# Two gate projections as seven-product block problems, branches and merge with tokens as rows, and the mixer put in a new order

## The chip, the cores and the metric

The kernel runs on one core of a Trainium2 chip. The metric is device time in microseconds for one execution. In a profile, PE is TensorE's matmuls, PEld its weight loads, DVE is VectorE, ACT is ScalarE, POOL is GpSimd and SP is SyncE, which here only issues DMAs.

## The reference

Two layers (`DEPTH = 2`) of a streaming encoder over 512 tokens of width 1024, all in float32. Each layer is a token mixer and then a SwiGLU FFN, both with a residual and a layer norm behind them. The mixer, cut to what the change touches:

```python
h = jnp.einsum('bsd,de->bse', x, w_in[l])
rq, rk, rv, rg, cq, ck, cv, dq, dk, dv, gates = jnp.split(h, splits, axis=-1)   # gates: 3 x 1024 columns
o_a = _retention(rq, rk, rv, rg, ...)          # 4 heads, values 256 wide: 1024 columns
o_b = _chunk_attention(cq, ck, cv, ...)        # 8 heads of 64: 512 columns
o_c = _diff_attention(dq, dk, dv, ...)         # 4 heads of 2 x 64: 512 columns
g = sigmoid(gates + b_merge[l])                # one gate per branch and channel
merged = g_a * (o_a @ w_branch_a[l]) + g_b * (o_b @ w_branch_b[l]) + g_c * (o_c @ w_branch_c[l])
x = layer_norm(ALPHA * x + merged @ w_out[l])
```

Here the heads' shapes and the slices of `gates` are abridged. The gate projection is the widest piece: three matrices of 1024 x 1024 on 512 tokens. The kernel takes the sigmoid as (tanh(z/2) + 1)/2, and folds the factor 1/2 into a later copy.

## The kernel before

**Precision.** Every float32 operand is carried as a pair (`Pair`): a high part in float32r (ACT's cast) and the remainder (DVE's subtraction). One product is three matmuls (`mm3`, lines 121 to 124): high x high, high x low, low x high. A matmul has 128 x 128 stationary and up to 512 moving columns.

**Weights.** A weight block of 2048 columns per partition (1 MB) is loaded by SP into one of four staging slots (`wst`), cast by ACT (L154, L312), its remainder taken by DVE (L155, L319), into one of three slots for split weights (`wsp`). `run_items` walks a list of items written out by hand; `AHEAD = 3` blocks are fetched ahead of the item that runs.

**Items and gaps.** An item is a pair of weight requests and a function that issues its matmuls; the groups written behind it are lists of small steps, one list run at each call of `between()`, which the items make between their output tiles. The steps are the DVE, ACT and attention work: `s_q` (quarter sums), `s_r1` to `s_r3` (retention), `s_c1` to `s_c3` (chunk attention), `s_d0` to `s_d4` (differential attention). A planner orders each engine's queue by its own costs, with the program's order as priority; `keep_in_program_order` and `issue_after` bind single instructions.

**Two forms of projection.** The plain form, `proj_T`, makes a tile with 128 output channels as rows and 512 tokens as columns, in 24 matmuls for a depth of 1024. The block form, `u_two`, takes a weight matrix of 1024 x 1024 as 2 x 2 blocks of 512, the activations as halves of tokens by halves of depth, and forms the result from seven block products, named m1, m2, y, v, x, g, h, instead of eight, each 24 matmuls; its output has tokens as rows. Some products take plain quarters of the activations (m1, m2, h), the others sums of quarters, which `Quarters.left` (y and x) and `Quarters.right` (v and g) prepare from `xf` for four tiles k (`s_q(k)`: the tiles `sa` and `s12`, `sb` and `s43`). Weights are summed as well: `ahead_a` loads a block and has POOL's DMA add a second onto it, `ahead_c` the same; the classes `Close` and `Early` differ in how the other sums are made on DVE (L251, L257, L280). Before the change the block form serves the values `CV`/`DV` (`w`), two pairs of retention values and gates (`p`, `q`), the output projection (`o`) and the FFN.

**Gates and merge before.** The three gate matrices are in the plain form: `u_gate(br, i)` makes two tiles of channels; `gate_done` takes tanh with the bias as a per-partition scalar (L1121). Ten of the 24 tiles of a layer (`EARLY`) are parked in DRAM and come back later. `u_branch(br, i)` makes two tiles of channels of a branch's projection and merges them (L1154, L1158) into `acc[d]`, which has channels as rows, just what the output projection wants as its activation. Its quarter sums are `s_mleft` and `s_mright`.

**Order in a layer.** Layer 0 starts with `u_first` (retention's first queries and keys, and gate tiles 0 and 1, six tiles), two gate items, then `w`'s products. Layer 1 starts with m1 and m2 of `w`, whose plain quarters need no sums, while the previous layer's norm is turned; then `u_first`, with the steps `natural` (two operations on each half of a token tile's residual row, L579 and L580) and `s_q` in its gaps, two gate items, and then `w["y"]`. Behind that come `p` and `q`, and then attention steps in the gaps of branch, gate and query/key items. Gate items of 48 matmuls stand all along the mixer.

## Time and profile before

| | |
|---|---|
| time, median of 3 runs | 1864.18 us (1863.9 to 1864.31) |
| profiled execution: span | 1862.2 us, 2.0 us under the median; its own time beyond the span is not recorded |
| PE, DVE, ACT, POOL busy | 99%, 75%, 53%, 7% of the span |
| matmuls | 8772 |
| mean granted TensorE clock | 0.999 |
| moved by DMA | 302.89 MB, 163 GB/s in the mean |

"Busy" is the share of the span in which an engine has at least one instruction under way. A row of a group gives the line, the engine, the operation, the tiles written and read, the shapes and the count; then busy time and mean duration in ns; then the idle time of the engine just before, and what ended it. A matmul's duration overlaps its neighbours', so what one more matmul costs is the distance between two starts. Layer 0's mixer runs from 0 to about 586 us, its FFN to about 940, layer 1's mixer to about 1513.

### The profile page before, as it was taken

Reading aid. Unit: us, or ns where it says so; the run is one execution under the profiler, and the core shown is the slowest. Engines: PE = TensorE matmul, PEld = TensorE weight load, DVE = VectorE, ACT = ScalarE, POOL = GpSimd, SP = SyncE. Lnnn points to the kernel's source line nnn. Section 1 sums busy time; section 2 is a strip of 40 time slices with the busy share of each in tenths; the row PEclk is TensorE's granted clock in tenths of the full one; section 3 lists DMA queues with packets and bytes.
Section 4 is the critical chain, followed back from the end, with each engine's and each line's share of the span. In section 5 each row is a group of like instructions: output and inputs, shape, how many; then the busy total and the mean of one; then the engine's idle time right before and its main releaser. Section 6 shows DMA issues by size and latency. Waiting matters only on the chain.

```text
span 1862.2 us, 23357 instructions
## 1 busy us (share of the span) xinstructions
PE 1852.4 (99%) x8772; PEld 1547.1 (83%) x8772; DVE 1391.9 (75%) x2124; ACT 990.1 (53%) x1590; POOL 131.1 (7%) x151
## 2 busy tenths in 40 slices
PE   9999999999999999999999999999999999999998
PEld 8888888888888888888888888888888888888887
DVE  6867756677679777888686777566775897778886
ACT  5555545576545445554354545546665464455540
POOL 2000000000001100010010000000000011000100
PEclk9999999999999999999999999999999999999999
DMA  9685444332456777797376844433325477777871
GB/s 285 189 262 152 124 139 133 95 121 75 121 167 166 179 198 182 202 220 205 129 227 186 257 115 143 152 110 106 113 68 147 137 181 183 198 198 198 202 197 46
DMA packets 235426, 302.89 MB, mean 163 GB/s; under 512 B 8757, under 2 KB 127633, under 8 KB 235313
## 3 DMA queue, kind: packets, MB, share of 16 engines
q1 hardware_dynamic: 205888, 244.09, 40.7%
q0 software_dynamic: 29280, 57.05, 17.6%
q8 instruction: 69, 1.13, 0.2%
q14 instruction: 45, 0.36, 0.1%
q10 hardware_dynamic: 144, 0.26, 0.0%
HBM read 279.29 MB, written 22.07 MB: 162 GB/s over the span
## 4 chain that ended last, share of the span: by engine, by line
PE 97%; DVE 2%; issue 0%; ACT 0%; POOL 0%; DVEq 0%; POOLq 0%
PE pt L122 15%; PE pt L123 15%; PE pt L124 15%; PE pf L124 14%; PE pf L122 14%; PE pf L123 14%; PE ptr L487 1%; PE psc L458 1%; PE pco L1002 1%; PE psc L457 1%; PE ph L1365 1%; PE pdo L1074 1%; DVE wl L155 1%; PE pro L124 1%; PE pro L123 1%; PE pro L122 1%
## 5 line engine op out<-in xcount | busy, mean ns | idle before, releaser
L319 DVE TENSOR_TENSOR wl<-st,wh 128x2048 fp32r<-128x2048 f32 (+1 forms) x143 | 320.5, 2244 | 118.5 <-ACT wh L312 117.9
L122 PE MATMUL pt<-xTh,wh 128*128 128x512 f32 x960 | 377.3, 394 | 0.0
L123 PE MATMUL pt<-xTl,wh 128*128 128x512 f32 x960 | 374.0, 390 | 0.4 <-DVE xTl L112 0.4
L124 PE MATMUL pt<-xTh,wl 128*128 128x512 f32 x960 | 374.2, 390 | 0.0
L312 ACT CAST wh<-st 128x2048 fp32r<-128x2048 f32 x140 | 267.3, 1912 | 194.0 <-PE pf L124 97.0
L155 DVE TENSOR_TENSOR wl<-st,wh 128x1024 fp32r<-128x1024 f32 (+2 forms) x186 | 200.2, 1093 | 48.6 <-ACT wh L154 35.2
L154 ACT CAST wh<-st 128x1024 fp32r<-128x1024 f32 (+2 forms) x186 | 172.2, 949 | 115.9 <-PE pt L123 56.1
L124 PEld LDWEIGHTS pt<-xTh,wl 128*128 128x128 f32 x960 | 180.2, 188 | 38.0
L123 PEld LDWEIGHTS pt<-xTl,wh 128*128 128x128 f32 x960 | 180.4, 188 | 37.0 <-DVE xTl L112 0.8
L122 PEld LDWEIGHTS pt<-xTh,wh 128*128 128x128 f32 x960 | 180.7, 188 | 36.5 <-ACT xTh L106 0.2
L122 PE MATMUL pf<-wh,xTh 128*128 128x512 f32 x336 | 132.0, 393 | 0.2
L124 PE MATMUL pf<-wh,xTl 128*128 128x512 f32 x336 | 131.6, 392 | 0.3
L123 PE MATMUL pf<-wl,xTh 128*128 128x512 f32 x336 | 130.9, 390 | 0.0
L122 PE MATMUL pf<-wh,s12h 128*128 128x512 f32 x256 | 100.7, 393 | 0.0
L122 PE MATMUL pf<-wh,s43h 128*128 128x512 f32 x256 | 99.8, 390 | 0.0
L123 PE MATMUL pf<-wl,s12h 128*128 128x512 f32 x256 | 99.8, 390 | 0.0
L123 PE MATMUL pf<-wl,s43h 128*128 128x512 f32 x256 | 99.7, 389 | 0.0
L124 PE MATMUL pf<-wh,s43l 128*128 128x512 f32 x256 | 99.4, 389 | 0.0
L124 PE MATMUL pf<-wh,s12l 128*128 128x512 f32 x256 | 99.2, 390 | 0.0
L809 ACT COPY tc<-pf 128x512 f32<-128x512 f32 x84 | 48.4, 589 | 80.6 <-PE pf L124 77.4
L124 PEld LDWEIGHTS pf<-wh,xTl 128*128 128x128 f32 x336 | 63.1, 188 | 15.4 <-DVE xTl L112 2.5
L122 PEld LDWEIGHTS pf<-wh,xTh 128*128 128x128 f32 x336 | 63.1, 188 | 14.0 <-issue 1.0
(329 smaller groups left out, 3666.7 us busy)
## 6 DMA issues: line engine op xcount, KB each, us to landing
st<-in_w_in SPq DMA_DIRECT2D x53, 1024.0 KB, 5.7
st<-in_w_ffn_in SPq DMA_DIRECT2D x38, 1024.0 KB, 5.6
st<-in_w_in SPq DMA_DIRECT2D x48, 512.0 KB, 5.1
st<-in_w_ffn_out SPq DMA_DIRECT2D x22, 1024.0 KB, 7.0
st<-in_w_ffn_in POOLq DMA_DIRECT2D x20, 1024.0 KB, 10.8
st<-in_w_ffn_out POOLq DMA_DIRECT2D x16, 1024.0 KB, 9.0
st<-in_w_in POOLq DMA_DIRECT2D x12, 1024.0 KB, 11.6
st<-in_w_ffn_in SPq DMA_DIRECT2D x24, 512.0 KB, 5.3
```

Of the source, the lines that this page charges most:

```text
L122: nc.tensor.matmul(ps, lh, rh, start=start, stop=False, skip_group_check=onto)
L123: nc.tensor.matmul(ps, lh, rl, start=False, stop=False, skip_group_check=onto)
L124: nc.tensor.matmul(ps, ll, rh, start=False, stop=stop, skip_group_check=onto)
L154: return [nc.scalar.copy(self.hi[:, a:b], self.st[:, a:b]), nc.vector.tensor_sub(self.lo[:, a:b], self.st[:, a:b], f(self.hi[:, a:b]))]
L155: nc.vector.tensor_sub(self.lo[:, a:b], self.st[:, a:b], f(self.hi[:, a:b]))]
L312: nc.scalar.copy(self.hi, st)
L319: nc.vector.tensor_sub(self.lo[:, k], self.st[:, k], f(self.hi[:, k]))
L457: nc.tensor.matmul(ps[:, :w], self.q[j][:, n], self.k[j][:, :w], start=True, stop=False)
L458: nc.tensor.matmul(ps[:, :w], self.q[j][:, n], self.kl[j][:, :w], start=False, stop=True)
L487: nc.tensor.transpose(ps[:, o + P * (nt - mt):o + P * (nt - mt) + P], E[pk][:, c + P * mt:c + P * mt + P], ident)
L809: nc.scalar.copy(t[to, j], ps)
L1002: nc.tensor.matmul(*x, start=mt == 0 and x is hi, stop=mt == NT - 1 and x is hi)
```

## The change

Gate matrices 0 and 1 go into the block form (`u_gates`, seven products each), with a bias row added at the copy; their tanh tiles have tokens as rows. Gate 2 and the three branches are made in `strips`: the activation is the stationary operand, 512 weight columns move, and the result has tokens as rows. All 24 tanh tiles of a layer go to DRAM and return at the merge. Merged tiles are turned by 32 transposes per layer (`s_merged`), and the output projection's sums are taken behind that (`s_msums`). `u_first` loses its gate block; in layer 0 and layer 1 the two gate items ahead of `w["y"]` make room for m1 and m2 of the first gate; `vectors`, `lam`, `v_back` and the split of `ob` move; `held` tells the fetch loop that strips keep a block longer.

```diff
-                while at <= i or (at < len(items) and sum(map(len, ready)) < AHEAD):
+                while at <= i or (at < len(items) and held + sum(map(len, ready)) < AHEAD):
...
-            return [([wcols(c, 256)], KT) for c in (RQ, RK, GATE)], fn
+            return [([wcols(c, 256)], KT) for c in (RQ, RK)], fn
...
                 def use(j, ps):
                     t[to, j] = g(name="t" + to)
-                    nc.scalar.copy(t[to, j], ps)
+                    if base:
+                        nc.vector.tensor_add(t[to, j], ps, base[to])
+                    else:
+                        nc.scalar.copy(t[to, j], ps)
...
             def h(j, ps):
+                if base:
+                    c, ps = ps, g(name="th")
+                    nc.vector.tensor_add(ps, c, base["c11"])
                 left_done(2 + j, ps)
...
+        def gate_done(br, hf, t, c):
+            nc.scalar.activation(c, c, AF.Tanh, scale=0.5)
+            th[br, t, hf] = dram.tile([P, 512], F32, name=f"th{l}_{br}_{t}_{hf}")
+            nc.sync.dma_start(th[br, t, hf], c)
...
+        def u_gates(kind, br):
+            hv = kind(W, 0, 4, (GATE + D * br, GATE + D * br + 512))
+            return u_two(hv, xq, functools.partial(gate_done, br, 0), functools.partial(gate_done, br, 1), Rows(br))
+
+        def strip(act, ks, wt, t, ps=None, stop=True):
+
+            start, sl = ps is None, slice(P * t, P * t + P)
+            ps = bank("pn") if start else ps
+            for i, k in enumerate(ks):
+                mm3(ps, act[k].hi[:, sl], act[k].lo[:, sl], wt.hi[:, i], wt.lo[:, i],
+                    start and i == 0, stop and i == len(ks) - 1)
+            return ps
...
+        def merge(br, t, hf, ps):
+            s = g(name="th")
+            nc.sync.dma_start(s, th.pop((br, t, hf)))
+            nc.vector.scalar_tensor_tensor(s, s, 1.0, ps, op0=ALU.add, op1=ALU.mult)
+            if (t, hf) in acc:
+                nc.vector.tensor_add(acc[t, hf], acc[t, hf], s)
+            else:
+                acc[t, hf] = s
...
+        def s_merged(half, *ks):
+
+            def fn():
+                for k in ks:
+                    ps = bank("pm")
+                    for hf in range(2):
+                        for j in range(2):
+                            o = 256 * hf + P * j
+                            nc.tensor.transpose(ps[:, o:o + P], acc[2 * half + j, hf][:, P * k:P * k + P], ident)
+                    r = raw[half, k] = g(name="mr")
+                    nc.scalar.activation(r, ps, AF.Copy, scale=0.5)
...
+        def s_msums(*ks):
+
+            def fn():
+                for k in ks:
+                    a, b, y = raw.pop((0, k)), raw.pop((1, k)), raw.pop(("y", k))
+                    pr, gr = Pair("mx"), HalfPair("mg")
+                    nc.vector.tensor_sub(y[:, A2], y[:, A2], a[:, A2])
+                    nc.vector.tensor_add(y[:, B2], y[:, A2], a[:, B2])
+                    split(pr, y)
+                    mq[k].put("x", pr, A2)
+                    mq[k].put("v", pr, B2)
+                    nc.vector.tensor_sub(a[:, A2], a[:, A2], b[:, A2])
+                    split(gr, a[:, A2])
+                    mq[k].put("g", gr, A2)
...
+        ga, gb = u_gates(Early, 0), u_gates(Close, 1)
...
         if l == 0:
-            start = [(u_first(),), (u_gate(0, 1), [s_q(0), s_q(1)], [s_q(2), w["a"]]), (u_gate(0, 2), [s_q(3)], [w["c"]]),
-                     (w["m1"],), (w["y"],), (w["v"],), (w["m2"], [lam])]
+            start = [(u_first(), [w["a"]], [s_rows(0)]), (w["m1"], [vectors, s_q(0)], [s_q(1)]), (w["m2"], [s_q(2)], [w["c"]]),
+                     (ga["m1"], [s_q(3)]), (ga["m2"], [lam])]
         else:
             turned, natural = ([functools.partial(fn, i) for i in range(4)] for fn in hooks[l])
             start = [(w["m1"], [ret_tables], turned[:2]), (w["m2"], turned[2:]),
-                     (u_first(), [natural[0]], [natural[1]], [natural[2]], [natural[3], w["a"]], [s_q(0)]),
-                     (u_gate(0, 1), [s_q(1)], [s_q(2)]), (u_gate(0, 2), [s_q(3)], [w["c"]]),
-                     (w["y"], [lam]), (w["v"],)]
+                     (u_first(), [natural[0]], [natural[1]], [natural[2], s_rows(0)], [natural[3], w["a"]]),
+                     (ga["m1"], [vectors, s_q(0)], [s_q(1)]), (ga["m2"], [s_q(2), w["c"]], [s_q(3), lam])]
...
+            (w["y"], [ga["a"]]), (w["v"],), (w["x"],), (w["g"],), (ga["y"],), (w["h"], [ga["c"]]), (ga["v"], [gb["a"], s_rows(1)]),
+            (ga["x"],), (gb["m1"],), (ga["g"],), (gb["y"],), (ga["h"], [gb["c"]]), (gb["v"], [p["a"]]), (gb["m2"], [s_dh(0)]), (gb["x"],),
+            (p["m1"],), (gb["g"],), (p["y"],), (gb["h"], [p["c"]], [s_r1(0)]), (p["v"], [s_dh(1)]), (p["m2"], [], [s_r1(1)]),
...
+            (u_cqk(2), [s_c2(1), s_c1(3)], [s_c3(1), s_c2(2)]),
+            a0[0], a0[1], (u_cqk(3), 2, [s_c3(3), s_c2(4)], [s_c3(4), s_c1(6)]), a0[2], a0[3],
+            a1[0], a1[1], (u_dqk(0), 2, [], [s_d0(0, 0)]), a1[2], a1[3],
+            (u_dqk(1), [s_d2(0), s_ob(0, 1)], [s_d0(1, 0), s_ob(2, 3)]), (u_chunked(0), [s_d3(0)], [s_d0(1, 1)]),
+            (u_dqk(2), [s_d4(0), s_d2(1)], [s_d0(2, 0)]), g1[0], g1[1],
+            (u_dqk(3), 2, [s_d4(1), s_d2(2)], [s_d0(3, 0)]), g1[2], g1[3],
+            (u_chunked(1), [s_d4(2), s_d2(3), o["a"]], [s_d3(3)]),
+            *quad(difference_strips(s_d4(3)), [], [[o["c"]]], [[], [s_merged(1, 0, 1)]], [[s_merged(1, 2, 3)]]),
+            (o["y"], [s_merged(0, 0, 1, 2, 3)]), (o["m1"], [s_msums(0)], [s_msums(1)]), (o["m2"], [s_msums(2)], [s_msums(3)]),
+            (o["v"],), (o["x"], [norm_rows]),
             (o["g"], [], [s_turned(0)]), (o["h"],),
```

More of the change, by code (lines that the diff above doesn't have):

```diff
@@ L588, in last_of, with item @@
         return [next(own) for _ in range(n)][-1]
[L590 to L592 removed]
+    def item(specs, fn, *groups, held=0):
+        items.append((specs, fn, groups, held))
     pending = []
@@ L931, in v_away, with v_back @@
             return done
-        def v_back(dst):
+        def v_back(dst, hf):
             def fn():
-                for k, away in list(dst.items()):
-                    dst[k] = g(F32R, "vhl")
-                    nc.sync.dma_start(f(dst[k]), away)
+                for t in range(NT):
+                    away, dst[t, hf] = dst[t, hf], g(F32R, "vhl")
+                    nc.sync.dma_start(f(dst[t, hf]), away)
             return fn
@@ new lines, in strip, with strips, part, fn @@
+        def strip(act, ks, wt, t, ps=None, stop=True):
[5 more added lines that the diff above has]
+            return ps
+        def strips(act, w, hf, use):
+            W2, ps = {}, {}
+            def part(k, ts):
+                def fn(*wt):
+                    if wt:
+                        W2[k], = wt
+                    for t in ts:
+                        if k == 0:
+                            ps[t] = strip(act, range(0, 4), W2[0], t, stop=False)
+                        else:
+                            use(t, hf, strip(act, range(4, 8), W2[1], t, ps.pop(t)))
+                return fn
+            c = slice(512 * hf, 512 * hf + 512)
+            one, two = [([w[0:512, c]], 4)], [([w[512:1024, c]], 4)]
+            return [(one, part(0, (0, 1)), 0), (two, part(1, (0, 1)), 1), ([], part(0, (2, 3)), 2), ([], part(1, (2, 3)), 1)]
```

202 lines of the change are left out of this document (91 added, 111 removed).

## The prediction

> **What bounds the kernel now.** I read the page first (busy shares and the chain that ended last), then the busy time in stretches of my own choice, then the instructions in order of time of PE and DVE round the stage that the change rebuilds.
>
> ```profile
> span 1862.2 us, 23357 instructions
> ...
> PE 1852.4 (99%) x8772; PEld 1547.1 (83%) x8772; DVE 1391.9 (75%) x2124; ACT 990.1 (53%) x1590; POOL 131.1 (7%) x151
> ...
> PE 97%; DVE 2%; issue 0%; ACT 0%; POOL 0%; DVEq 0%; POOLq 0%
> ```
>
> TensorE is the bound: it is busy 99% of the span and carries 97% of the chain. A matmul that goes is worth its spacing, as long as its operands stay ahead of PE. Whether they do is a question of stretches (columns: stretch, length, then busy time and count of PE, PEld, DVE, ACT, POOL, the clock, the DMA share and GB/s):
>
> ```profile
> 29.53:67.23 37.70, 37.70 (x168) 31.24 (x167) 31.29 (x46) 20.87 (x28) 2.64 (x2) 1.00 0.75 207
> 942.18:1002.57 60.39, 59.98 (x263) 48.64 (x261) 51.71 (x80) 29.52 (x45) 8.66 (x14) 1.00 0.73 209
> 235.50:551.00 315.50, 315.43 (x1590) 266.77 (x1589) 214.60 (x468) 183.47 (x396) 16.04 (x22) 1.00 0.41 122
> 551.00:561.90 10.90, 10.90 (x50) 9.03 (x49) 10.90 (x13) 5.50 (x5) 0.00 (x0) 1.00 0.32 97
> 69.00:240.00 171.00, 170.86 (x804) 143.16 (x803) 129.21 (x151) 92.76 (x134) 8.20 (x8) 1.00 0.62 183
> ```
>
> PE has no hole in any of them. In the first two, the openings of layers 0 and 1 up to the last quarter sum, DVE is busy 83% and 86%. That matters because the first product that needs quarter sums (`w["y"]`) cannot finish before DVE has written `s12` for the fourth tile. The rows in time, layer 0 and then layer 1:
>
> ```profile
> 60.49 0.39 PE L122 MATMUL pf<-wh,xTh 128*128 128x512 f32 x1
> ...
> 65.93 0.39 PE L122 MATMUL pf<-wh,s12h 128*128 128x512 f32 x1
> ```
> ```profile
> 29.53 0.69 DVE L424 TENSOR_TENSOR rot<-pt,cosr 128x512 f32<-128x512 f32 x1 [3.54 <-DMA cosr<-in_rope_ret]
> ...
> 66.62 0.68 DVE L112 TENSOR_TENSOR s12l<-sa,s12h 128x512 fp32r<-128x512 f32 x1
> ```
> ```profile
> 997.85 0.39 PE L122 MATMUL pf<-wh,s12h 128*128 128x512 f32 x1
> ...
> 1002.71 0.50 PE L124 MATMUL pf<-wh,s12l 128*128 128x512 f32 x1
> ```
> ```profile
> 1001.97 0.68 DVE L112 TENSOR_TENSOR s12l<-sa,s12h 128x512 fp32r<-128x512 f32 x1
> ```
>
> In layer 1, PE enters `y` at 997.85, runs all that does not need the fourth tile, and takes its low part at 1002.71, just after DVE wrote it (1001.97 + 0.68). The slack is nil. In layer 0 the fourth tile is finished at 67.3 and `y` would use it at 65.93 + 9 matmuls = 68.0. So in both layers the work that PE has ahead of `y` now is just enough to cover DVE. This decides my forecast.
>
> **The change, part by part.** *Matmuls.* Between 60.49 and 65.93 lie the 24 matmuls of one product: 5.44 us, 0.2267 each. A gate matrix is now 8 column tiles x 8 x 3 = 192 matmuls; as seven products of 24 it is 168. Two matrices, two layers: 96 fewer, -21.8 us. The third gate, the branches and the output projection keep their counts (2 halves x 4 token tiles x 8 x 3 = 192, as before).
>
> *Transposes of merged tiles.* 4 x 2 x 4 = 32 per layer, 64 in all.
>
> ```profile
> 253.57 1.04 PE L912 MATMUL prt<-ident,ro 128*128 128x128 f32 x8
> 254.37 0.48 PE L122 MATMUL pt<-xTh,wh 128*128 128x512 f32 x1
> ```
>
> Eight take 0.80 us from start to start: 64 cost +6.4 us, all on PE. PE's own account is thus -15.4 us. I would expect 8772 - 96 + 64 = 8740 matmuls.
>
> *The opening of each layer.* This is the part on the path. Layer 0 now has 264 matmuls ahead of `y` (six tiles of `u_first`, two gate items, `w["m1"]`); after, 192 (four tiles, and m1 and m2 of `w` and of the first gate). That is 72 x 0.2267 = 16.3 us less cover: PE reaches `y` at 49.6. Layer 1 goes from 288 to 192, 21.8 us less: at 976.1. From there 18 of the 24 matmuls can run without the fourth tile (as the order of layer 1 shows today), 4.1 us more: 53.7 and 980.2. What has DVE to do until then? Its prices:
>
> ```profile
> L319 DVE TENSOR_TENSOR wl<-st,wh 128x2048 fp32r<-128x2048 f32 x137 | 313.2, 2289 | 118.5 <-ACT wh L312 117.9
> ...
> L155 DVE TENSOR_TENSOR wl<-st,wh 128x1024 fp32r<-128x1024 f32 x144 | 173.3, 1220 | 34.4 <-ACT wh L154 29.6 <-PE ptr L487 4.4
> ...
> L580 DVE TENSOR_TENSOR z<-z,bc 128x512 f32<-128x512 f32 x24 | 16.5, 686 | 0.3
> ...
> L814 DVE TENSOR_TENSOR tc<-tc,pf 128x512 f32<-128x512 f32 x28 | 19.1, 683 | 17.3 <-PE pf L124 17.3
> ...
> L112 DVE TENSOR_TENSOR vhl<-tc,vhl 128x256 fp32r<-128x256 f32 x24 | 9.0, 418 | 1.4 <-ACT vhl L106 1.4
> ```
>
> Layer 0, stretch 29.53 to 67.23, 31.3 us busy. Out go the weight remainders of two gate items (four halves, 4.9) and, as done earlier or later now, those of m1 and v:
>
> ```profile
> 30.87 1.22 DVE L155 TENSOR_TENSOR wl<-st,wh 128x1024 fp32r<-128x1024 f32 x1
> ...
> 35.56 1.21 DVE L155 TENSOR_TENSOR wl<-st,wh 128x1024 fp32r<-128x1024 f32 x1
> ...
> 42.53 2.29 DVE L319 TENSOR_TENSOR wl<-st,wh 128x2048 fp32r<-128x2048 f32 x1
> ...
> 64.42 2.28 DVE L319 TENSOR_TENSOR wl<-st,wh 128x2048 fp32r<-128x2048 f32 x1
> ```
>
> together 9.5. In come the remainders of m2, of the gate's m1 and m2 (3 x 2.29), the two adds of `w["m2"]` and its four value remainders (2 x 0.68 + 4 x 0.42), and the first bias add (0.68): 10.6. So 32.4 us of work from 29.53: done at 61.9 with no idle time, at 68.3 with the 6.4 us of idle time that the stretch has now (mostly waits of 0.7 us for ACT's cast of a high part). I take half, 65.1: PE waits 11.4 us (8.2 to 14.6).
>
> Layer 1, stretch from 942.18, 51.7 us busy. The fetch of x moves behind, two gate items go:
>
> ```profile
> 955.79 1.22 DVE L155 TENSOR_TENSOR wl<-st,wh 128x1024 fp32r<-128x1024 f32 x1
> ...
> 967.27 1.22 DVE L155 TENSOR_TENSOR wl<-st,wh 128x1024 fp32r<-128x1024 f32 x1
> ...
> 994.90 2.28 DVE L280 TENSOR_TENSOR st<-st 128x2048 f32<-128x2048 f32 x1
> ...
> 998.04 0.22 DVE L725 TENSOR_TENSOR lp<-lv 128x64 f32<-128x64 f32 x1
> ...
> 998.76 0.29 DVE L727 TENSOR_REDUCE ls<-lp 128x2 f32<-128x128 f32 x1
> ...
> 999.76 2.29 DVE L319 TENSOR_TENSOR wl<-st,wh 128x2048 fp32r<-128x2048 f32 x1 [0.71 <-ACT wh L312]
> ```
>
> Four halves (4.9), the 2.28 and the 2.29, and `lam` with `hb` (three rows from 998.04 to 998.76 and 0.2: 0.9): -10.4. The remainder of the gate's m2 and four bias or m2 adds come in: 2.29 + 4 x 0.68 = +5.0. That leaves 46.3: 988.5 without idle time, 997.2 with today's 8.7. Half: 992.9, a wait of 12.7 us (8.3 to 17.0). It could be less than that: the 16 operations on the residual rows (`natural`, 0.69 each, 11 us) stand ahead of `s_q` in the program and need not. As the program's order puts them first today, I leave them there. Both waits: 24.1 us.
>
> *After `y`.* Seven products of a gate load DVE with 9 x 2.29 + 14 x 0.68 = 30.1 us in 38.1 us of PE, 79%, no more than the 83% and 86% above: nothing. DMA: gates now bring 15 MB where four gate items brought 4, and 4 MB of tanh tiles go out instead of 2: 13 MB at 183/0.62 = 295 GB/s is 44 us on top of 0.62 x 171 = 106, in 171 + 33 us of PE: share 0.74, covered by prefetch. The row loads on SP, `v_back` in halves, and `vectors` (ten small POOL transfers and one transpose, behind POOL's first sum of blocks now) hide there too; uncovered, each would cost one landing, some 6 us. One path is tight: a block summed in flight.
>
> ```profile
> st<-in_w_in SPq DMA_DIRECT2D x53, 1024.0 KB, 5.7
> ...
> st<-in_w_in POOLq DMA_DIRECT2D x12, 1024.0 KB, 11.6
> ...
> rows<-in_ln_g POOLq DMA_DIRECT2D x4, 4.0 KB, 6.3
> ```
> ```profile
> L312 ACT CAST wh<-st 128x2048 fp32r<-128x2048 f32 x140 | 267.3, 1912 | 194.0 <-PE pf L124 97.0 <-PE pt L123 39.0 <-issue 37.0
> ...
> L1154 DVE SCALAR_TENSOR_TENSOR th<-th,pt 128x512 f32<-128x512 f32 x48 | 32.0, 681 | 15.6 <-PE pt L124 9.9 <-DMA th<-th 4.2 <-issue 1.5
> ```
>
> Load, sum, cast (1.9) and remainder (2.3) take 21.5 us. The gates' `ahead_a` is issued half a product plus three products ahead of its `y`, 19.0 us (five with a gate item between, 32, for `p` today). Zero to 2.5 us for each of four; it can be issued earlier where staging slots allow. I take 0.
>
> *Attention.* 43.5 us of gate items per layer leave the stretch 235.5 to 551, and about 4 us of DVE with them: (214.6 - 4)/(315.5 - 43.5 + 3) = 77%, against 68%. Every merge now waits for a tanh tile to come back (48 loads, 20 of them before); such waits cost DVE 4.2 us in all; two and a half times that is still hidden behind 23% of idle time. Nothing; locally up to 2 us.
>
> *Before the output projection.* DVE is busy for all of 551.0 to 561.9 already. The sums of merged tiles (`s_msums`: per tile 3 x 0.42 + 0.69 + 0.42 = 2.4) can start only once the last branch tile is merged: 9.5, plus 4 x 0.69, two remainders, last merges and adds, some 21 us in three products and 16 transposes of 17.9 us; the last tile is needed 4.1 us later. 0 to 3 us per layer; I take 1.
>
> **Sum.** Span 1862.2 - 15.4 + 24.1 + 2 = 1872.9; the runs' median, 1864.18, lies 2.0 us above the profiled span, so 1875.
>
> **A rule weighed.** At the start of the kernel, the same transposes run slower:
>
> ```profile
> 1.49 3.68 PE warm L630 x16
> ```
>
> Sixteen take 3.4 us from 1.49 to 4.91, 0.21 each against 0.10 above. The Trainium skill, "TensorE: Matmul & The Clock Gate", Part 1, says that after about 3.4 us without work the array falls to half clock, and needs as long under load to recover. By it, each of my two waits would cost up to 1.7 us more (an estimate from that page), the sum 1878; nothing above rests on this, as no wait of that length stands in this trace.
>
> **The rivals.**
> 1. *DVE gets to the quarter sums in time, faster.* The order puts `s_q` ahead of the residual rows and of weight remainders not yet due. Layer 1 then has 988.5 - 11 = 977.5, before 980.2; layer 0 would need 8 us of other work put behind. With no wait: 1864.2 - 15.4 = 1849, to 1856 with layer 0's. For: DVE has 6 to 9 us idle in each stretch and nothing forces the rows first. Against: today's order already ends with no slack. It decides when both waits, with the tails, come to less than 11.7 us. Chance 0.31.
> 2. *The waits eat the gain exactly.* No idle time on DVE: 8.2 + 8.3 = 16.5, so 1864.2 + 1.1 = 1865. Chance 0.13.
> 3. *Transfers as well.* Four late summed blocks, 10 us, tails of 3 us and the slow restart: about 1890. Chance 0.12.
>
> **How the numbers follow.** The main case has 0.44 and gives 1875; its own range is 1865 to 1884 (waits of 16.5 to 31.6, tails of 0 to 4). About 4 us (0.2%) is what can be told from no change: faster means below 1860.5, which is rival 1 alone, 0.31; rival 2 is the same, 0.13; slower is 0.44 + 0.12 = 0.56. The range of eight in ten reaches to rival 1 on one side and to rival 3 on the other: 1848 to 1890.
>
> **What would show it.** PE in order of time: the first `s12` product in layer 0 near 50 us and near 976 (shifted by layer 0's balance) in layer 1, each followed by a hole of 8 to 17 us ending on DVE's `s12l`; 8740 matmuls; the chain with DVE well above 2%; no hole near the gates' own `y`. If PE stays at 99% the forecast is wrong at the order of DVE's work; if holes lie elsewhere, at what I set to nothing.

## The result, and the profile after

The changed kernel takes 2035.56 us (median of four runs, 2034.14 to 2039.85), the kernel before 1864.04 us beside it: a ratio of 1.0925 (1.0909 to 1.0940). That is 171.5 us slower, far outside my range.

The head of the page after, its row of the granted clock and the chain's shares:

```profile
span 2032.3 us, 23555 instructions
...
PE 1891.2 (93%) x8740; PEld 1566.6 (77%) x8740; DVE 1480.5 (73%) x2193; ACT 1012.3 (50%) x1594; POOL 139.0 (7%) x157
...
PEclk8799999998888999999998999999988999999999
...
PE 75%; DVE 10%; ACT 6%; DMA 5%; issue 3%; POOL 0%; SPq 0%; DVEq 0%; ACTq 0%; POOLq 0%
```

8740 matmuls, as counted. But PE's share fell from 99% to 93%, a quarter of the chain is no longer PE's, and the clock is down in patches. PE's waits over the whole run (what, by whom; total us, times, longest):

```profile
PE psc L455 <- ACT ks L104: 67.6, 10, 9.4
PE pf L120 <- ACT s12h L104: 17.2, 5, 7.1
PE pf L121 <- DVE wl L317: 9.8, 7, 2.3
PE pf L120 <- ACT wh L310: 8.7, 3, 5.3
PE pm L1227 <- DVE th L1172: 5.7, 2, 2.9
PE pf L120 <- DVE rot L422: 4.8, 2, 4.6
```

(Helper lines are two lower than before: L120 to L122 are `mm3`, L104 and L110 the cast and the remainder of a pair.) The largest wait by far, 67.6 us, is one that I never named: the scores of the differential attention (`psc`) waiting for the casts of their own keys (`ks`).

From the starts of neighbouring matmuls I made an account. At full clock a 512-column matmul follows the one before by 0.2267 us. An excess of over 0.32 us I call a gap; a smaller one I call half clock. Not all of the second is that: the kernel before has 13.2 us of it at a mean granted clock of 0.999. What counts is the amount above the kernel before, and by the clock's own record 36.6 us of the changed kernel's small excesses lie in stretches granted half clock, none of the kernel before's. The span grew by 170.1: matmuls and transposes -15.4 (as predicted), gaps +147.5 (0.9 before, 148.4 after), half clock +38.2 (13.2 before, 51.4 after). By stage (0 to 210, 210 to 720, 720 to 1215, 1215 to 1720 us), gaps / half clock in us, for the kernels that matter below:

| kernel | time | opening 0 | mixer 0 to norm | opening 1 | mixer 1 to norm |
|---|---|---|---|---|---|
| before | 1864.0 | 0.3 / 3.0 | 0.0 / 3.9 | 0.6 / 2.3 | 0.0 / 3.8 |
| changed | 2035.6 | 33.1 / 14.0 | 47.2 / 16.1 | 21.7 / 7.4 | 46.4 / 13.2 |
| e1_scores_later | 1991.6 | 39.0 / 14.6 | 24.0 / 12.5 | 23.1 / 6.8 | 25.2 / 12.4 |
| e5_d_spread | 1986.4 | 35.0 / 14.4 | 23.3 / 13.7 | 21.5 / 6.9 | 21.4 / 13.4 |
| e7_strips_ahead | 2002.4 | 37.7 / 11.3 | 28.3 / 17.5 | 19.5 / 6.7 | 28.3 / 17.1 |
| e15_no_pool_sums | 1971.0 | 23.8 / 10.6 | 28.9 / 14.6 | 11.1 / 3.7 | 30.2 / 16.4 |
| e10_one_gate | 1964.3 | 25.6 / 5.7 | 21.3 / 12.6 | 10.3 / 8.7 | 21.3 / 12.8 |
| e9_plain_gates | 1913.9 | 7.6 / 4.4 | 15.3 / 8.5 | 0.0 / 2.2 | 14.4 / 7.2 |

In the changed kernel 38.3 and 37.6 us of the mixers' gaps lie in the differential attention itself. The first such gap, PE and then VectorE and ScalarE in order of time (start, duration, instruction, idle time ahead and its releaser):

```profile
452.40 0.39 PE L122 MATMUL pt<-xTh,wl 128*128 128x512 f32 x1
460.94 0.80 PE L455 MATMUL psc<-ks,qs 128*128 128x512 f32 x1 [8.15 <-ACT ks L104]
```
```profile
456.57 0.69 DVE L422 TENSOR_TENSOR rot<-pt,cosd 128x512 f32<-128x512 f32 x1 [1.14 <-ACT sw L420]
457.18 0.68 DVE L423 TENSOR_TENSOR sw<-sw,sind 128x512 f32<-128x512 f32 x1
457.78 1.22 DVE L153 TENSOR_TENSOR wl<-st,wh 128x1024 fp32r<-128x1024 f32 x1
458.92 0.68 DVE L424 TENSOR_TENSOR rot<-rot,sw 128x512 f32<-128x512 f32 x1
```
```profile
454.20 2.34 ACT L420 COPY sw<-pt 32x512 f32<-32x512 f32 x4
456.56 1.04 ACT L152 CAST wh<-st 128x1024 fp32r<-128x1024 f32 x1
459.63 2.54 ACT L104 CAST ks<-rot 64x512 fp32r<-64x512 f32 x4 [2.02 <-DVE rot L424]
```

PE starts `u_dqk(0)`'s last matmul at 452.40. Copying that tile, its rotary and its casts take until 460.9, on engines that are not full (DVE 105 of 170 us in this stretch), and the next PE instruction is the score that needs it. In the kernel before, other items stood between the keys and their score, ScalarE and then PE:

```profile
374.07 2.54 ACT L106 CAST ks<-rot 64x512 fp32r<-64x512 f32 x4 [2.14 <-DVE rot L426]
...
388.73 0.45 PE L457 MATMUL psc<-ks,qs 128*128 128x512 f32 x1
```

The changed kernel has eight such gaps of 7.7 to 9.6 us, four in each layer.

### The profile page after: what moved, and what is told of

Same layout as the page of the kernel before. It is cut to its first block, busy times and chain, and to the rows that moved or that the text cites. A ratio compares the mean times of both kernels' runs of the same rounds, so it can differ in the third digit from the quotient of the medians.

```text
span 2032.3 us, 23555 instructions
## 1 busy us (share of the span) xinstructions
PE 1891.2 (93%) x8740; PEld 1566.6 (77%) x8740; DVE 1480.5 (73%) x2193; ACT 1012.3 (50%) x1594; POOL 139.0 (7%) x157
## 4 chain that ended last, share of the span: by engine, by line
PE 75%; DVE 10%; ACT 6%; DMA 5%; issue 3%; POOL 0%; SPq 0%; DVEq 0%; ACTq 0%; POOLq 0%
PE pf L121 13%; PE pf L120 13%; PE pf L122 13%; PE pt L120 5%; PE pt L121 5%; PE pt L122 5%; PE pn L120 4%; PE pn L121 4%; PE pn L122 4%; DMA st<-in_w_in 3%; DVE wl L317 2%; ACT sw L420 2%; ACT wh L310 2%; PE psc L455 1%; PE psc L456 1%
## 5 line engine op out<-in xcount | busy, mean ns | idle before, releaser
L317 DVE TENSOR_TENSOR wl<-st,wh 128x2048 fp32r<-128x2048 f32 (+1 forms) x174 | 384.8, 2215 | 151.8 <-ACT wh L310 151.2
L310 ACT CAST wh<-st 128x2048 fp32r<-128x2048 f32 x168 | 319.8, 1909 | 259.3 <-PE pf L122 92.4
L120 PE MATMUL pt<-xTh,wh 128*128 128x512 f32 x576 | 226.8, 395 | 3.4 <-DVE qs L112 2.6
L121 PE MATMUL pt<-xTl,wh 128*128 128x512 f32 x576 | 225.0, 391 | 1.9 <-DVE xTl L651 1.9
L122 PE MATMUL pt<-xTh,wl 128*128 128x512 f32 x576 | 225.2, 391 | 0.0
L120 PE MATMUL pf<-wh,xTh 128*128 128x512 f32 x432 | 172.0, 398 | 10.9 <-ACT wh L310 5.9
L122 PE MATMUL pf<-wh,xTl 128*128 128x512 f32 x432 | 169.8, 393 | 0.0
L120 PE MATMUL pf<-wh,s12h 128*128 128x512 f32 x288 | 119.2, 415 | 20.7 <-ACT s12h L104 17.2
L120 PEld LDWEIGHTS pt<-xTh,wh 128*128 128x128 f32 x576 | 109.0, 190 | 25.9 <-issue 2.8
L121 PEld LDWEIGHTS pt<-xTl,wh 128*128 128x128 f32 x576 | 108.7, 189 | 24.3 <-DVE xTl L651 2.2
L122 PEld LDWEIGHTS pt<-xTh,wl 128*128 128x128 f32 x576 | 108.5, 188 | 22.7
L122 PE MATMUL pf<-wh,s12l 128*128 128x512 f32 x288 | 115.7, 406 | 0.0
L120 PE MATMUL pf<-wh,s43h 128*128 128x512 f32 x288 | 112.8, 392 | 1.4 <-ACT tc L795 1.4
L122 PE MATMUL pf<-wh,s43l 128*128 128x512 f32 x288 | 112.1, 389 | 0.0
L455 PE MATMUL psc<-ks,qs 128*128 128x512 f32 (+3 forms) x128 | 45.3, 368 | 67.6 <-ACT ks L104 67.6
L120 PEld LDWEIGHTS pf<-wh,xTh 128*128 128x128 f32 x432 | 82.2, 190 | 30.6 <-ACT wh L310 6.9
L121 PEld LDWEIGHTS pf<-wl,xTh 128*128 128x128 f32 x432 | 82.3, 191 | 24.1 <-DVE wl L317 7.7
## 6 DMA issues: line engine op xcount, KB each, us to landing
st<-in_w_ffn_in POOLq DMA_DIRECT2D x20, 1024.0 KB, 10.9
```

Source lines behind the costliest of these rows:

```text
L120: nc.tensor.matmul(ps, lh, rh, start=start, stop=False, skip_group_check=onto)
L121: nc.tensor.matmul(ps, lh, rl, start=False, stop=False, skip_group_check=onto)
L122: nc.tensor.matmul(ps, ll, rh, start=False, stop=stop, skip_group_check=onto)
L310: nc.scalar.copy(self.hi, st)
L317: nc.vector.tensor_sub(self.lo[:, k], self.st[:, k], f(self.hi[:, k]))
L455: nc.tensor.matmul(ps[:, :w], self.q[j][:, n], self.k[j][:, :w], start=True, stop=False)
```

## The experiments

### The differential attention

**e1_scores_later.** Each first half of the scores goes one stretch of PE work later, what follows it too.

```diff
-(u_dqk(0), 2, [], [s_d0(0, 0)]), a1[2], a1[3],
-(u_dqk(1), [s_d2(0), s_ob(0, 1)], [s_d0(1, 0), s_ob(2, 3)]), (u_chunked(0), [s_d3(0)], [s_d0(1, 1)]),
+(u_dqk(0), 2), a1[2], a1[3],   # s_d0(0, 0), s_d0(0, 1) in a1's gaps
+(u_dqk(1), [s_d2(0), s_ob(0, 1)], [s_ob(2, 3)]), (u_chunked(0), [s_d3(0)], [s_d0(1, 0)]),
```

> The changed kernel with the differential attention's scores of head h, part 0, taken out of the query/key item that makes them and put one stretch of TensorE work later (5 to 11 us), the steps that follow them shifted with them; nothing else. Theory A (scores issued straight behind their own rotary find nothing to run meanwhile): the eight holes of about 8 us in front of `psc` (66 us) and the half-clock stretches behind them (some 17 us) go, 2035 to about 1952 (1945 to 1970). Rival B (VectorE is full in this stretch, so the wait only moves to a later step): over 2010, with new holes of the same sum between 450 and 620 us.

Measured 1991.56 us, 44 less than the changed kernel, between theory A and rival B. PE's waits in this run:

```profile
PE ptr L485 <- DVE dE L1041: 20.9, 6, 5.5
PE pf L120 <- ACT s12h L104: 17.1, 5, 7.1
PE pf L120 <- ACT wh L310: 16.3, 4, 6.2
```

The 67.6 us row is gone, but a part moved one step on: the transposes of `s_d2` now wait for the merge of the two halves (`dE`), since that pair had come too close.

**e5_d_spread.** The whole chain is spread: each `u_dqk(h)` one item earlier, 8 to 11 us of other matmuls between all steps of a head.

```diff
+(u_dqk(0), [s_c3(6), s_c2(7)], [v_back(dv, 0), s_c3(7)]), a1[0], a1[1],          # a1[1]: s_d0(0, 0)
+(u_dqk(1), 2, [s_ob(0, 1)], [s_d0(0, 1), s_ob(2, 3)]), a1[2], a1[3],             # a1[3]: s_d2(0), s_d0(1, 0)
+(u_dqk(2), [s_d3(0)], [s_d0(1, 1)]), (u_chunked(0), [s_d4(0)], [s_d2(1), s_d0(2, 0)]), ...
```

> The changed kernel with the items of the differential attention in another order: each u_dqk(h) stands one whole item earlier, every s_d0(h, 0) comes at least 10.9 us of other matmuls behind its own u_dqk(h), and s_d0(h, 1), s_d2, s_d3, s_d4 keep at least 10.9, 10.9, 8 and 10.9 us of matmuls between them. No work is added or left out. Theory A (PE only waits because the steps of one head stand too close, DVE has room: it was busy 105 us of 170 there): the gaps of this stretch, 38.3 and 37.6 us with 10.8 and 8.6 us at half clock behind them, fall below 8 us a layer, and the time to 1950 to 1965. Theory B (the two gate matrices were the cover, and without them this stretch is too short for DVE's and ACT's steps whatever their order): gaps stay at 15 us a layer or more as in the run with the scores one stretch later, time 1980 to 1995.

Measured 1986.43, ratio 1.0658 (1.0627 to 1.0689): 49 less than the changed kernel. The time lies in theory B's range; the gaps from 450 to 620 us, 12.9 against 38.3 us, lie between the two. About half of the mixers' gaps (93.6 us, now 44.7) are gone by order alone. The other half stays in many small waits (`ptr` for `dE` 11.9 us in 8, longest 3.4).

**e4_keep_warm.** 64 unused transposes ahead of each `s_d0(h, 0)`.

```diff
+if j == 0:
+    keep = bank("keep")
+    for _ in range(64):
+        nc.tensor.transpose(keep[:, :P], ident, ident)
```

> The changed kernel with 64 extra transposes of the identity (6.4 us at 0.10 each, output unused) ahead of each of the eight scores that TensorE waits for. Theory A (an idle TensorE is granted half clock and pays for it behind the hole): the extra work runs in the holes and the slow stretches behind them go, 12 to 19 us less, 2016 to 2023. Rival B (the lower granted clock costs no time of its own): 2035, or more by what of the 51 us of extra work does not fit the holes.

Measured 2031.1 (2027.97 to 2034.24). Busy time in layer 0's stretch, the changed kernel and this one (PE, PEld, DVE, ACT, POOL, clock, DMA share, GB/s):

```profile
450.00:620.00 170.00, 134.17 (x621) 112.04 (x620) 105.03 (x223) 88.81 (x198) 9.94 (x12) 0.87 0.39 118
```
```profile
450.00:620.00 170.00, 161.38 (x901) 139.45 (x900) 105.60 (x224) 91.53 (x202) 9.94 (x12) 0.97 0.39 118
```

512 more PE instructions, some 51 us at 0.1, at no cost. So the gaps are time in which PE has nothing it may run. The clock in the stretch rose from 0.87 to 0.97. The time can hardly be told from the changed kernel's 2034.14 to 2039.85, and is nearer to rival B; the trace says more. From the last matmul ahead of the first wait to that ahead of the fourth, this run needs 111.1 us in each layer, the changed kernel 115.9 and 115.1: nearly 9 us less at half clock, in theory A's direction. Layer 0's opening, which the edit doesn't touch, took 4.6 us longer in this execution.

### The two gate matrices as cover

**e9_plain_gates.** Everything as changed, but gates 0 and 1 as plain strips: gate 0's ahead of the opening's sums, gate 1's in the differential attention, with the steps around them in another order.

```diff
-ga, gb = u_gates(Early, 0), u_gates(Close, 1)
+*quad(gate_strips(0, 0), ...), *quad(gate_strips(0, 1), ...), (w["y"], [lam]), ...
+(u_dqk(1), ...), *quad(gate_strips(1, 0), [[]], [[s_d2(0), s_d0(1, 0)]], [[]], [[s_d3(0), s_d0(1, 1)]]), (u_dqk(2), ...), *quad(gate_strips(1, 1), ...)
```

> Half of the change undone: branches, merge and transposed merged tiles as in the changed kernel, but the gate matrices of branches 0 and 1 as plain strips of 96 matmuls (as branch 2's are), not as block problems by seven products. Branch 0's two quads of strips stand ahead of w["m1"] (layer 0) or w["y"] (layer 1), branch 1's two among the items of the differential attention, and the opening's blocks in the order of the kernel before. It has 96 matmuls of 0.2267 us (21.8 us) more than the changed kernel, and 64 transposes (6.4 us) more than the kernel before. Theory A (the two matrices were the cover of the opening and of the differential attention, and putting them into the block sequence took it away): nearly all gaps and the half clock behind them go, with 5 to 15 us left at the merge: 1870 to 1895, 140 to 165 below the changed kernel for 21.8 us more work. Theory B (the losses come from the form with tokens as rows, its merges, its strips and its order): 1950 or more.

Measured 1913.85, ratio 1.0269 (1.0239 to 1.0299): 122 below the changed kernel with 21.8 us more matmuls in it. Theory A's direction, its size missed by some 20 us. The page's head:

```profile
span 1913.4 us, 23648 instructions
...
PE 1872.2 (98%) x8836; PEld 1560.8 (82%) x8836; DVE 1422.8 (74%) x2162; ACT 993.0 (52%) x1598; POOL 130.4 (7%) x149
...
PEclk9999999999999999999999999999999999999999
```

The openings are clean but for 6 us of gaps in the first 50. What remains above before, 51.2 us of span, is 6.4 of transposes, 36.4 of gaps and 9.4 of half clock (together 1.0 more than the span grew, the account's error): steps of the two attentions (in an order of mine) and the turning of merged tiles (`pm` waits 2.9 us per layer).

**e10_one_gate.** As e9, but with gate 0 as blocks and gate 1's first quad of strips ahead of them.

```diff
+*quad(gate_strips(1, 0), [[s_q(0)]], [[s_q(1)]], [[s_q(2)]], [[s_q(3)]]), (w["m1"],), (w["m2"], [], [w["c"]]), (ga["m1"],), (ga["m2"], [lam])
```

> Between the two: only branch 0's gate matrix as blocks (behind w's, as in the changed kernel), branch 1's as plain strips, its first quad ahead of the opening's blocks and its second in the differential attention. 48 matmuls (10.9 us) fewer than with both plain. Theory A (cover is what counts, and one matrix can be spared): the sum of the run with both plain, less 10.9, plus 10 to 25 us of gaps in the openings: 1870 to 1905. Theory B (the block sequence itself makes the opening wait, by VectorE's additions and evictions ahead of the fourth s12 and by its summed blocks): the openings keep 40 us or more of their 55 us of gaps and some 15 us of half clock: 1910 to 1930.

Measured 1964.29: 50 above the run with both plain, for 10.9 us less work. One matrix as blocks adds 28 us of gaps and 8 of half clock in the openings, 13 and 10 in the mixers. Theory B was nearer, though the time is past its range. The largest wait:

```profile
PE pf L120 <- DVE th L1169: 17.1, 2, 13.4
```

A product waits for the bank of a strip whose eviction stood in VectorE's queue behind two rounds of `s_q` and two sums of blocks.

### The openings: what makes the fourth quarter sum late

In layer 1 PE's waits up to `y` are for `s12`. In layer 0 they are so only in part (0 to 210 us of the changed kernel):

```profile
PE pf L120 <- ACT wh L310: 5.9, 2, 5.3
PE pf L120 <- ACT s12h L104: 5.8, 2, 3.2
PE pf L120 <- DVE rot L422: 4.8, 2, 4.6
```

The longest wait of the first row stands at 39.2 us: ScalarE's cast of a weight block came behind a step of `lam`, for which ScalarE had stood idle for 18.0 us. That of the third, at 61.1, is for a bank that the rotary had not yet read. Both lie ahead of `y`, which PE reached at 73.0.

Edits that move or take out VectorE's work here changed little, or made it slower.

**e2_lam_behind** binds `lam`'s VectorE steps behind the VectorE instruction before them in the program.

```diff
+with tc.issue_after(last_of(nc.vector)):
+    lam_of()
```

> The changed kernel with layer 0's `lam` bound behind the VectorE instructions issued before it, so that it cannot be put ahead of the rotary in VectorE's and ScalarE's queues. Theory A (in layer 0 both queues stand from 28 to 39 us for the `lv` rows, whose loads now start at 27 us and stand behind POOL's first sum): rotary starts 10 us sooner, 8 to 14 us less in all, 2021 to 2027. Rival B (my prediction's ledger alone sets the end of the quarter sums): less than 3 us.

Measured 2036.45: no change, and no test, as `lam` still ran ahead of the rotary, at 39.5 to 42.3 us.

**e6_vectors_first** issues layer 0's small loads ahead of POOL's first summed block, as before.

```diff
-(u_first(), [w["a"]], [s_rows(0)]), (w["m1"], [vectors, s_q(0)], [s_q(1)])
+(u_first(), [vectors, w["a"]], [s_rows(0)]), (w["m1"], [s_q(0)], [s_q(1)])
```

> The changed kernel with layer 0's vectors (the small loads that POOL issues) put ahead of w["a"], POOL's first summed block, as in the kernel before. Nothing else. Theory A (lam's VectorE steps hold the rotary of layer 0 back because their four loads are issued behind POOL's first summed block, at 26.7 to 34.9 us): the loads are issued about 10 us earlier, rotary starts 8 to 12 us earlier, so does y, and the time is 2023 to 2028. Theory B (what is late for the fourth s12 is VectorE's own work in the opening, which is the same): below 3 us, time 2032 to 2036.

Measured 2029.65 (2027.75 to 2031.56): 6 less, between the theories. In the changed kernel, POOL and then VectorE:

```profile
33.32 0.56 POOL L705 DMA_DIRECT2D lv<-in_da_lambda_k  x1 [5.98 <-DMA st<-in_w_in]
```
```profile
39.30 0.22 DVE L715 TENSOR_TENSOR lp<-lv 128x64 f32<-128x64 f32 x1 [13.12 <-DMA lv<-in_da_lambda_k]
```

VectorE stood idle for 13.1 us on a small load that POOL could issue only once its summed block was through. With e6's edit the rotary starts at 38.1 instead of 42.9. The gaps ahead of `y` fell from 25.3 to 21.7 us, the half clock by 4; those behind `y` rose by 7.

**e3_rows_behind** puts the residual rows of layer 1 behind `y`; **e11_no_rows** leaves their 16 VectorE operations out; **e12_sq_first** puts the four `s_q` into `u_first`'s gaps.

```diff
-(u_first(), [natural[0]], [natural[1]], [natural[2], s_rows(0)], [natural[3], w["a"]])     # e3: natural in the gaps of w["v"] to ga["y"]
-hooks[l + 1] = (...), (lambda t: x2["n"].natural(t))
+hooks[l + 1] = (...), (lambda t: x2["n"].as_is(t))                                         # e11
+(u_first(), [s_q(0), natural[0]], [s_q(1), natural[1]], [s_q(2), natural[2], s_rows(0)], [s_q(3), natural[3], w["a"]])   # e12, layer 0 alike
```

> The changed kernel with layer 1's sixteen residual-row operations (`natural`) taken from the gaps of `u_first` into those of the products v, x, g and the next y, behind the quarter sums. Theory A (VectorE's order decides the wait at layer 1's y): the fourth `s12` about 10 us sooner, 10 to 16 us less with the clock, 2019 to 2026. Rival B (other work takes the place, or the rows now held longer keep slots from others): within 4 us of 2035.

> The changed kernel with layer 1's residual rows of the opening written as they are: the 16 VectorE operations of natural (0.69 us each, 11.0 us) are left out, so the rows lack the norm's scale and bias. Theory A (in layer 1 VectorE's dense sequence up to the fourth s12 sets when w["y"] starts): y starts 9 to 11 us earlier, the opening's gaps fall from 21.7 to about 12 us: 2024 to 2027. Theory B (y waits for something else there, a summed block or the order on PE): within 3 us of the changed kernel.

> The changed kernel with the four s_q steps in the four gaps of u_first in both layers (they stood in the gaps of the block products behind it). No work is added or left out. Each s_q goes from VectorE to ScalarE and back twice (4.3 us a round in the fastest rounds of the changed kernel, four rounds 17 us), and on ScalarE its casts stand behind casts of weight blocks (wh) which wait for a slot that TensorE frees. Theory A (this chain behind the queue of the casts makes the fourth s12 late): the fourth s12 is there about 17 us behind the last rotary, some 12 to 20 us earlier in each layer; gaps of the openings fall from 33 to about 15 us and from 22 to below 10 us: 2035 less 20 to 40, 1995 to 2015. Theory B (the openings are short of VectorE time whatever the order, as the run without the rows suggests): within 8 us of the changed kernel, 2027 to 2040.

Measured 2049.95, 2038.26 (2032.45 to 2044.08) and 2051.06: none faster, theory A fallen three times; that e3 and e12 came out 14 and 16 us slower, neither theory had. The four `s12` remainders of layer 0 in before, changed, e12 and e9 (durations, first to last start), and of layer 1 in the changed kernel and e11:

```profile
L112 DVE TENSOR_TENSOR s12l<-sa,s12h x4: 684/692/693, 50.3 to 66.6; 128x512 fp32r<-128x512 f32 x4
```
```profile
L110 DVE TENSOR_TENSOR s12l<-sa,s12h x4: 685/692/693, 74.7 to 90.5; 128x512 fp32r<-128x512 f32 x4
...
L110 DVE TENSOR_TENSOR s12l<-sa,s12h x4: 685/692/693, 1081.0 to 1096.4; 128x512 fp32r<-128x512 f32 x4
```
```profile
L110 DVE TENSOR_TENSOR s12l<-sa,s12h x4: 685/686/693, 52.2 to 91.8; 128x512 fp32r<-128x512 f32 x4
```
```profile
L110 DVE TENSOR_TENSOR s12l<-sa,s12h x4: 685/691/691, 56.9 to 77.4; 128x512 fp32r<-128x512 f32 x4
```
```profile
L110 DVE TENSOR_TENSOR s12l<-sa,s12h x4: 685/692/693, 1084.9 to 1100.2; 128x512 fp32r<-128x512 f32 x4
```

In e12 the first tile comes 22 us earlier and the fourth not at all: the rotary rounds went behind instead. In layer 1 `u_first` starts at 1038.7 in the changed kernel and 1046.0 in e11, so the fourth tile comes 57.7 and 54.2 us behind it; 59.8 in before, 53.7 in e9, 53.9 in e12. So in these five, whatever the order, and with 11 us of VectorE's work taken out, the rotary and the `s_q` rounds of layer 1, which go from VectorE to ScalarE and back in turn, need some 54 to 60 us. What differs is PE's work in that time: from `u_first` to `y` it had 54.4 us before (240 matmuls), has 65.3 in e9 (288) and 32.6 in the changed kernel (144). For the wait on `s12`, what was lost is cover.

**e13_sq_spread** and **e14_all** add the spread order of e5 to e12, and then e6's edit.

> The s_q steps in u_first's gaps and the spread order of the differential attention together. Theory A (separate causes, gains add): 49 us below the run with the s_q steps alone, as the spread order gave on the changed kernel. Theory B (a wait removed in one stage comes back in the next): less than 35 us below it.

> As the run before it, and layer 0's small loads (vectors) ahead of POOL's first summed block. Theory A (with the s_q chain out of the way, layer 0's opening starts with the rotary, which waits for lam): 5 to 12 us below the run without. Theory B (the rotary then waits for u_first's own last products and for casts of weights, as in the run with the vectors alone): within 4 us of it.

Measured 1994.06 and 1992.32. The spread order gives 57 here (49 on the changed kernel): the attention's loss and the openings' are separate. The small loads give nothing more.

**e7_strips_ahead** puts cover back: e5's order, and `gate_strips(0)`, 21.8 us of matmuls, ahead of `w["y"]` in both layers. **e8_three** adds e6's edit.

```diff
+*early, (w["y"], [ga["a"]]), (w["v"],), ...      # early = quad(gate_strips(0), ...), taken from behind u_cqk(1)
```

> The order of the run with the differential attention spread, and in both layers gate_strips(0), 96 matmuls that need only xT and two bias rows, moved from the first attention to a place ahead of w["y"]; the steps of the first attention are drawn together over the items that remain. Theory A (the opening lacks 16 to 22 us of TensorE cover, nothing else): gaps of the openings fall from 33 to about 15 us in layer 0 and from 22 to below 5 us in layer 1, half-clock time with them; the first attention, with 21.8 us less beside it, may give 0 to 10 us of it back: 25 to 40 us below the run with the spread order alone. Theory B (VectorE is what the opening runs on; the strips' weights and additions, about 7 us of VectorE by the like rows, come ahead of the fourth s12 and move y by as much, and the first attention loses its cover): within 8 us of the run with the spread order.

> All three edits together: spread order, layer 0's vectors ahead of POOL's first summed block, gate_strips(0) ahead of w["y"]. Theory A (three separate losses): the gains add, 8 to 12 us below the run without the vectors' edit, about 1905 to 1925. Theory B (in layer 0 the strips already fill the time in which VectorE waits for lam's loads): the same as the run without the vectors' edit within 3 us.

Measured 2002.36 and 1997.87: 16 and 11 above e5. Neither theory of e7 had it slower, and e8's gain of 4.5 us on e7 lies between its two. The first attention, now without those strips, got 9.8 and 11.2 us of gaps (5.4 and 4.2 in e5). And the openings kept theirs, with 21.8 us more work in each: ahead of `y` they fell by 4.9 and 6.5, behind `y` they rose by 7.7 and 4.6. No gap of e7's openings ends on `s12` any more, so the cover did its work there. PE waits instead for banks that VectorE has not emptied (`tc`) and for casts of weight blocks (`wh`), here from 0 to 210 us:

```profile
PE pn L120 <- DVE tc L800: 11.1, 2, 7.3
...
PE pf L120 <- ACT wh L310: 6.7, 2, 5.5
```

The strips' own additions also stand in VectorE's queue: layer 1's fourth `s12` comes 62.9 us behind `u_first` here.

### Behind `y`

All on e7's order, but for the last. **e15_no_pool_sums** leaves out POOL's summed loads of the gates' blocks, **e16_no_vector_sums** VectorE's sums of them; **e17_strips_act_stores** lets ScalarE issue the stores of `th`, and **e18_act_stores** does that on the changed kernel.

```diff
+hv.more = lambda *_: None                         # e15
+if self.sums:                                     # e16, around the tensor_add in v and in x or m2
-nc.sync.dma_start(th[br, t, hf], c)
+nc.scalar.dma_start(th[br, t, hf], c)             # e17, e18
```

> The run with gate_strips(0) ahead of w["y"], with POOL's summed loads of the two gate matrices' blocks left out (two of 1024 KB for each matrix and layer): those blocks are used as loaded, so these gates come from other weights. Theory A (summed loads that land late, about 10 us each behind a load of the same size, make PE wait behind y): the gaps behind y, 15 us in layer 0 and 11 us in layer 1 in the run with the strips ahead, fall below 5 us each: 2002 less 15 to 22 with their half clock, 1980 to 1988. Theory B (something else orders these blocks): within 5 us of 2002.

> The same base, with VectorE's three sums of blocks left out for each gate matrix (2.29 us each, and each holds its block's slot until it has run), POOL's kept; these gates come from other weights too. Theory A (VectorE's sums and what waits for them: a summed block's load waits in SyncE's queue for the slot): 2002 less 8 to 20. Theory B: within 5 us of 2002.

> The same base, with gate_done's stores of th issued by ScalarE, which has just written them, instead of SyncE; all work is done. Theory A (loads of blocks stand in SyncE's queue behind stores that wait for their tiles; in the run with the strips ahead that queue waits 30 us for th and tc in layer 0's opening): loads start earlier, 2002 less 8 to 20. Theory B (loads wait for free slots anyway): within 5 us of 2002.

> The changed kernel with the stores of th issued by ScalarE, nothing else. Theory A (SyncE's queue): 2035 less 5 to 15, in the openings behind y and in the first attention. Theory B: 2030 to 2040, as the slots set the loads.

(In e16 it is two sums for each matrix, not the three that its expectation names.) Measured 1971.04, 1993.39, 2004.16 and 2040.34: -31, -9, +2 and +5, each against the run it was made from. Busy time behind `y` in layer 0, e7 and then e15 (columns as above):

```profile
100.00:210.00 110.00, 96.06 (x410) 77.48 (x409) 71.92 (x61) 45.37 (x47) 6.40 (x5) 0.97 0.82 236
```
```profile
100.00:210.00 110.00, 108.18 (x479) 89.09 (x477) 84.52 (x69) 54.12 (x55) 2.58 (x2) 1.00 0.72 223
```

Gaps behind `y` fall from 15.3 to 2.1 us (layer 0) and from 11.4 to 3.1 (layer 1). With cover put ahead of `y`, the row of block products runs into blocks that POOL sums in flight. The trace of e7 shows the path in the longest of these gaps (7.2 us, up to 127.8): POOL issued its sum at 110.4, ScalarE sat idle for 9.0 us until it could cast that block at 122.3, and the eviction that PE waited for stood in VectorE's queue behind the block's remainder. e15 also moves 8.4 MB less; what that alone is worth no run shows. VectorE's sums are worth 9 us, the low end of theory A; the stores in SP's queue nothing that these runs can tell.

## Why the prediction was wrong

- **Matmuls and transposes, -15.4: right.** 8740 counted; PE's own work in the account fits the span to 0.2 us.
- **"Attention ... Nothing; locally up to 2 us": the step that failed.** It measured 75.9 us of gaps in the two differential attentions alone. I divided DVE's work by the stage's length and got 77%. The mean was near (from 450 to 620 us, 105.0 us of DVE beside 134.2 us of PE, 78%; 62% of the stretch as it came out), but it bounds no single wait. The limit is the distance, in PE work, from each `u_dqk(h)` to the score that needs it: a path of 8 to 9 us through two engines, with nothing between. The written order showed that.
- **The openings: near in layer 1, in layer 0 wrong in part.** I gave 12.7 and 11.4 us, both as waits for `s12`. In layer 1 three gaps of 11.9 us together end on `s12h`, out of 14.6 (and 4.2 of half clock) up to 1100 us. PE was at `y` as computed (1071.7, against 976.1 and a shift of 96.5), while the fourth `s12` came 57.7 us behind `u_first`'s start where my ledger, the sum of VectorE's work, had 50.7 and the kernel before 59.8; in the wait PE ran what it had of `y`, slowly. Layer 0 has 25.3 us of gaps up to 100 us, and by the account only 6.1 of them end on `s12h`. About as much (6.5) ends on a weight block that ScalarE cast late and 5.1 on banks held for the rotary, ahead of `y`: waits that the prediction doesn't have. The ledger started VectorE at 29.5, but the rotary came at 42.9. `vectors`, which had moved behind POOL's sum and which I named and priced at nothing, accounts for 4.8 of these 13.4 us (e6); what holds the rest is not shown. From there the fourth `s12` took 47.6 us where the ledger had 35.6. Adding busy times is no model of rounds that alternate between two engines.
- **"After `y` ... I take 0" (0 to 10): mis-sized.** 7.8 us in layer 0 and 7.1 in layer 1, from 100 and from 1100 on. e15 shows summed blocks as the cause with the strips ahead of `y`; for the changed kernel itself that is not shown.
- **Before the output projection, 2:** 12.9 us of gaps in the tails, 5.7 of it `pm` waiting for the last merges (`th`), a wait that I had put on `s_msums`.
- **The clock, 0 in the sum: mis-sized by 38.2 us** (36.6 by the clock's record). The rule that I weighed decided more than I let it; it is taken up in the last section.
- **Rivals.** None came; transfers (rival 3) were the nearest in kind, with the wrong place and a seventh of the size. The sum's terms after: -15.4, 54 in the openings, 76 in the differential attentions, 13 in the tails, 5 in the first attentions, 38 of half clock.

What is not settled: which part of e9's 122 us belongs to cover in the openings and which to the attention, as it puts back both and also has another order of the attention's steps, which alone was worth 49 us in e5; and how much of its remaining 50 us belongs to the tokens-as-rows form and how much to my order of its steps. No run beat the kernel before.

## What to carry to other kernels

When work is removed from a stage, list for every matmul that reads a vector engine's output how much PE work lies between its producer and itself, before and after; a mean busy share of 77% says nothing about a pair with nothing between. A path that goes back and forth between two engines has to be priced as a path, from a stretch of the trace where it runs alone, not as a sum of busy times. A matmul that covers such a path is worth more than its 0.2267 us: here, 21.8 us of them put back, together with a wider order of the attention's steps, made the kernel 122 us faster.

## What the runs showed of the hardware

The granted clock answered to gaps. PE at the second of the eight waits:

```profile
498.00 0.79 PE L455 MATMUL psc<-ks,qs 128*128 128x512 f32 x1 [9.42 <-ACT ks L104]
...
500.94 0.63 PE L121 MATMUL pn<-wl,obh 128*128 128x512 f32 x1
501.37 0.63 PE L122 MATMUL pn<-wh,obl 128*128 128x512 f32 x1
501.79 0.63 PE L120 MATMUL pn<-wh,obh 128*128 128x512 f32 x1
502.22 0.57 PE L121 MATMUL pn<-wl,obh 128*128 128x512 f32 x1
502.62 0.39 PE L122 MATMUL pn<-wh,obl 128*128 128x512 f32 x1
502.86 0.39 PE L120 MATMUL pn<-wh,obh 128*128 128x512 f32 x1
```

After a wait of 9.4 us the matmuls follow each other by 0.43 us, not 0.23, for some 4.4 us. Short gaps went both ways: those of 2.0 and 2.6 us at 129 and 142 us left 0.3 us of it together, while behind those of 2.2, 2.1 and 2.7 us at 21, 173 and 607 us it came to 1.3 to 2.0 us. The record grants half clock in stretches of 3.4, 6.8 or 10.2 us, but for the one at the span's end. The Trainium skill, "TensorE: Matmul & The Clock Gate", Part 1, has the array fall to half clock after about 3.4 us without work and recover after as long under load; the long waits agree with it, the short ones in part. I had weighed it as 1.7 us for each of two waits; with 12 gaps of over 3.5 us and shorter ones beside them the loss is 38.2 us more than before.
